# Output projection of an attention layer, halved by heads instead of by columns, with its first sums kept in place

## The chip, the cores and the metric

The kernel runs on one core of one Trainium2 chip. The metric is the device time of one execution in microseconds (us): the median of three runs. A profile of one further execution shows the engines: TensorE (PE; PEld is its weight load), VectorE (DVE), ScalarE (ACT), GpSimd (POOL) and SyncE (SP, which only issues transfers here).

## What is computed

A decoder trunk of two layers on 1024 tokens of width 1024. Layer 0 mixes tokens by a gated short convolution, layer 1 by sparse attention with 16 heads of 128. Behind each mixer stand a residual with layer norm and a mixture of 64 experts (one group of eight, then two experts of it), again with residual and norm. Cut to what matters here:

```python
for i in range(DEPTH):                        # 2
    if i % 2 == 0: m = short_conv_mixer(x, ...)
    else:          m = dsa_mixer(x, ...)      # ends in  o @ w_out,  o: (1024, 2048), w_out: (2048, 1024)
    x = layer_norm(DEEPNORM_ALPHA * x + m, ln1_g[i], ln1_b[i])
    f = hier_moe(x, router_wg[i], router_bg[i], router_we[i], router_be[i], w1[i], w3[i], w2[i])
    x = layer_norm(DEEPNORM_ALPHA * x + f, ln2_g[i], ln2_b[i])
```

## The kernel before

SBUF is an arena of 25 slots of 128 x 2048 numbers (1 MB); `take` and `give` hand them out first in, first out. The order of the work is written out by hand, per engine in program order. Tokens come in 8 tiles of 128.

Matrix products that decide the routing are made of three TensorE passes (`mm3`, L219 to L221): each operand is split into a rounded high part (ScalarE, L207) and the rest (a subtraction, L208, on VectorE or, if the call says so, on GpSimd).

The attention leaves its output in eight slots `Qs[t]`, one per tile, 16 heads of 128 each. The projection then runs over the columns of `w_out` in two halves n of 512, and in each half over the tiles t, in each tile over two head halves q of eight heads. `split_o` splits one head half of one tile (128 x 1024) into one of two buffers `os_[q]`; it is called for each (n, t, q), 32 times. `split_wo` splits the weights, 8 slots for a column half. The first pass (n = 0) keeps its products in `mA` by a ScalarE copy (L1811). The second pass (n = 1) is `mixer`, a generator that `mixer_ln_router` steps through: that function, which layer 0 uses too behind its convolution, loads the residual rows (L411, L414, L465, three buffers `rb`), adds the products (`part`, L427), normalizes the tile before (`norm`, L237 and L242 through `ln_apply`), writes it to DRAM (L444, issued by GpSimd), transposes it (`turn`, L421 and L422) for the router's logits (L557), chooses experts (`route_choice`, L572 to L626) and ranks tokens (`route_rank`, L654 to L687; `table_rows` and `table_slots`, L692 and L698). `fold_router` (L188 to L202) folds the norm's scale into the router's weights during the first tile. `ln_scale` and the line behind it (L230, L231, L433) are small GpSimd operations. Between its steps `prefetch` (L762, on SP) loads expert weights of 1 MB into the slots that are free.

The expert stage (`moe`) takes the experts in 32 pairs; L848 is the activation of a pair. Each layer's experts are 192 loads of 1 MB.

Of the kernel before, what the change touches and what calls it, by code (L numbers as in the profile page):

```python
# [23 lines left out]
F32 = mybir.dt.float32  # L24
# [4 lines left out]
AF = mybir.ActivationFunctionType  # L29
OP = mybir.AluOpType  # L30
# [3 lines left out]
P = 128  # L34
T = 1024
D = 1024
NT = T // P
# [8 lines left out]
ALPHA = 4.0 ** 0.25  # L46
# [3 lines left out]
HEADS = 16  # L50
# [13 lines left out]
MB, EO, EP = 4, -7, 4  # L64


class Net:
# [336 lines left out]
    def mixer_ln_router(self, l, x, mixer, done):  # L404
        nc = self.nc
        rs = [self.take() for _ in range(2)]
        self.rr = None
        *rb, tb = (self.slots[s][:, i * D:(i + 1) * D] for s in rs for i in range(2))
        rb = [rb[t % 3] for t in range(NT)]
        for t in range(2):  # L410
            nc.sync.dma_start(rb[t], x[t * P:(t + 1) * P])  # L411
        self.load_ln(self.i["ln1_g"][l], self.i["ln1_b"][l], nc.sync)
        self.load_router(l)
        nc.sync.dma_start(rb[2], x[2 * P:3 * P])  # L414
        self.route_open()

        def turn(t, h):
# [6 lines left out]
        def part(t, n, ap):  # L424
            s = slice(n * 512, (n + 1) * 512)
            r = rb[t]
            nc.vector.scalar_tensor_tensor(r[:, s], r[:, s], ALPHA, ap, op0=OP.mult, op1=OP.add)  # L427
            self.ln_stats(r, sts[t], n)
            if n:
                st = sts[t]  # L430
                for _ in self.ln_scale(st):
                    pass
                nc.gpsimd.tensor_mul(st[:, 14:15], st[:, 12:13], st[:, 15:16])  # L433
# [18 lines left out]
        last = NT - 1  # L452
        for t in range(NT):
            sts.append(self.small.tile([P, 16], F32, name="st", bufs=3))
            m = mixer(t)
            next(m)
            if t >= 1:
                next(fold, None)
                turn(t - 1, 1)
            g = [self.route_rank(t - 2)] if t >= 2 else []  # L460
            for r in g:
                some(r, FIRST)
            self.run(*([norm(t - 1)] if t >= 1 else []), *g)
# [51 lines left out]
        self.table_slots(t)  # L515
        self.close_slots()
        self.count_all()
        self.give(*rs, self.ln_slot, self.rt, self.rr)


    def route_open(self):
# [676 lines left out]
    def attention(self):  # L1198
        nc, sm, mm = self.nc, self.small, self.nc.tensor.matmul
        w_in, w_out = self.i["attn_w_in"][0], self.i["attn_w_out"][0]  # L1200
        S = self.slots
# [178 lines left out]
        Qs, Q = [], []  # L1380
# [251 lines left out]
        for k, (h, hh) in enumerate(order):  # L1632
# [66 lines left out]
        done = LEAD  # L1699
        raws = {}  # L1700

        def load_wo(n, i):
            r = raws[n, i] = self.take()
            nc.sync.dma_start(S[r].rearrange("p (j c) -> p j c", j=4),
                              w_out[i * 512:(i + 1) * 512, n * 512:(n + 1) * 512].rearrange("(j p) c -> p j c", p=P))

        wos, os_ = {}, []
        chunks = [(n, t, q) for n in range(2) for t in range(NT) for q in range(2)]

        def split_wo(n, i, qs=range(2), eng=None):  # L1710
            r = raws[n, i]
            v = S[r].rearrange("p (j c) -> p j c", j=4)
            for q in qs:
                s = wos[n, 2 * i + q] = self.take()
                o = S[s].rearrange("p (j a c) -> p j a c", j=2, a=2)
                self.split(v[:, 2 * q:2 * q + 2], o[:, :, 0], o[:, :, 1], eng)
            if 1 in qs:
                self.give(raws.pop((n, i)))

        def split_o(c, eng=None):  # L1720
            if c < len(chunks):
                _, t, q = chunks[c]
                self.split(S[Qs[t]][:, q * T:(q + 1) * T], S[os_[q]][:, :T], S[os_[q]][:, T:], eng)

        def project_ahead():

            self.give(*qs, *bs, *mcs[:2], pps[(len(items) - 3) % 3])
            load_wo(0, 2)
            os_.extend(self.take() for _ in range(2))
            split_o(0, nc.gpsimd)  # L1730
            yield
            for i in range(2):
                for q in range(2):
                    split_wo(0, i, (q,), nc.gpsimd if 2 * i + q < EP else None)
                    yield
            load_wo(0, 3)

# [3 lines left out]
        for i in range(len(items)):  # L1741
# [43 lines left out]
        mas = [self.take() for _ in range(2)]  # L1785
        mA = [S[mas[t // 4]][:, (t % 4) * 512:(t % 4 + 1) * 512] for t in range(NT)]
        state = {}

        def project(n, t, q, ks=range(8)):
            if q == 0 and 0 in ks:  # L1790
                state["pt"] = po.tile([P, 512], F32, name="po1")
            o = S[os_[q]]
            for k in (8 * q + k for k in ks):
                w = S[wos[n, k // 2]][:, (k % 2) * T:(k % 2 + 1) * T]
                hs = slice((k % 8) * P, (k % 8 + 1) * P)
                self.mm3(state["pt"], (o[:, :T][:, hs], o[:, T:][:, hs]), (w[:, :512], w[:, 512:]),
                         k == 0, k == HEADS - 1)
            return state["pt"]

        for t in range(NT):  # L1800
            for q in range(2):
                if t == 0 and q == 1:
                    split_wo(0, 2)
                    split_wo(0, 3)
                pt = project(0, t, q)
                split_o(2 * t + q + 1)
                if t == NT - 1:
                    self.give(*[wos.pop((0, 4 * q + i)) for i in range(4)])
                    split_wo(1, 2 * q)
                    split_wo(1, 2 * q + 1)  # L1810
            nc.scalar.activation(mA[t], pt, AF.Copy)  # L1811
            if t < 4:
                load_wo(1, t)

        split_o(2 * NT + 1)

        def mixer(t):
            c = 2 * (NT + t)
            project(1, t, 0, range(2))
            yield  # L1820
            project(1, t, 0, range(2, 8))
            split_o(c + 2, nc.gpsimd)
            if t == NT - 1:
                self.give(*[wos[1, i] for i in range(4)], os_[0])
            yield 0, mA[t]
            if t == 3:
                self.give(mas[0])
            elif t == NT - 1:
                self.give(mas[1])
                self.prefetch(1, 0, AHEAD[1][0])  # L1830
            project(1, t, 1, range(4))
# [8 lines left out]
        self.mixer_ln_router(1, self.xres, mixer, lambda: self.give(*[wos[1, i] for i in range(4, 8)], os_[1]))  # L1840
        ctx.close()


# [63 lines left out]
```

## Time and profile before

| | us |
|---|---|
| median of 3 runs | 2292.85 (2290.36 to 2293.92) |
| profiled execution | 2296.11 |
| its span in the profile | 2294.3 |
| TensorE busy | 2163.9 (94%) |
| VectorE busy | 1179.2 (51%) |
| ScalarE busy | 797.5 (35%) |
| GpSimd busy | 367.7 (16%) |

The profile counts time from the start of the span. Busy time of TensorE is modelled (its matmuls are pipelined), and the granted clock PEclk is a share of full speed, 2.4 GHz; a stretch at 0.83 has parts at 1.2 GHz. Of the span, the convolution's projection loop lies at 290 to 400, the experts of layer 0 at 430 to 910, the attention before 1540, the output projection at 1540 to 1772 (first pass to 1627), the rest of the routing to 1810 and the experts of layer 1 from there to the end.

### The profile page before, as it was taken

What the parts mean: (1) busy time and instruction counts of PE and PEld (TensorE: products, weight loads), DVE (VectorE), ACT (ScalarE), POOL (GpSimd) and SP (SyncE); (2) the same over time, 40 slices, a digit from 0 to 9 for tenths busy, and PEclk for the clock granted to TensorE, in tenths of its full rate; (3) what the DMA queues carried; (4) which work ended last, traced back from release to release, by engine and by line L of the source; (5) the groups of instructions that cost most, each with busy time, mean ns of one, the idle gap of its engine ahead of it and who ended that gap; (6) DMA issues with size and microseconds to landing.
All of it is one profiled execution on the core that took longest, in us unless ns stands there. A gap on an engine that the chain in (4) does not pass through costs nothing. (4 is left out here: it accounts for less than half of the span.)

```text
span 2294.3 us, 32929 instructions
## 1 busy us (share of the span) xinstructions
PE 2163.9 (94%) x12764; PEld 1597.5 (70%) x12764; DVE 1179.2 (51%) x2728; ACT 797.5 (35%) x1626; POOL 367.7 (16%) x435
## 2 busy tenths in 40 slices
PE   8999999799999998799998999999988799999997
PEld 6888888465555654677887899988766455655553
DVE  4333478433333334467888877772688333333333
ACT  3121211222222222356885877762321222222221
POOL 0000011100000001412332633230233100000001
PEclk9999999899999999899998999999988899999999
DMA  5113165699999997221211001010334899999994
GB/s 156 47 56 112 64 249 198 248 418 407 419 419 419 419 419 295 88 55 47 56 28 56 1 2 38 1 62 31 107 129 184 314 418 409 419 419 419 419 420 204
DMA packets 132692, 497.41 MB, mean 217 GB/s; under 512 B 18499, under 2 KB 64787, under 8 KB 82864
## 3 DMA queue, kind: packets, MB, share of 16 engines
q1 hardware_dynamic: 117648, 456.61, 50.6%
q0 software_dynamic: 8496, 34.20, 3.8%
q10 hardware_dynamic: 6384, 4.42, 0.7%
q8 instruction: 102, 1.67, 0.3%
q14 instruction: 62, 0.51, 0.1%
HBM read 474.60 MB, written 19.95 MB: 216 GB/s over the span
## 5 line engine op out<-in xcount | busy, mean ns | idle before, releaser
L840 PE MATMUL ph<-slot,slot 128*64 128x256 f32 x4096 | 456.3, 381 | 7.6 <-DVE nx L741 7.6
L840 PEld LDWEIGHTS ph<-slot,slot 128*64 128x64 f32 x4096 | 296.6, 138 | 183.4 <-issue 45.0
L871 DVE SCALAR_TENSOR_TENSOR slot<-rg,sgate,slot 128x512 fp32r<-128x512 f32 x128 | 96.1, 750 | 288.7 <-ACT slot L870 287.7
L866 PE MATMUL rg<-slot,slot 128*64 128x512 f32 x1024 | 233.8, 598 | 0.9 <-ACT slot L856 0.9
L207 ACT ACTIVATE slot<-slot 128x1024 fp32r<-128x1024 f32 (+3 forms) x169 | 139.5, 873 | 250.3 <-DVE slot L357 147.7
L208 DVE TENSOR_TENSOR slot<-slot,slot 128x1024 fp32r<-128x1024 f32 (+3 forms) x150 | 131.9, 918 | 149.5 <-ACT slot L207 149.5
L219 PE MATMUL ps<-slot,slot 128*128 128x512 f32 x512 | 202.7, 396 | 0.0
L221 PE MATMUL ps<-slot,slot 128*128 128x512 f32 x512 | 199.9, 390 | 0.0
L220 PE MATMUL ps<-slot,slot 128*128 128x512 f32 x512 | 199.8, 390 | 0.0
L219 PE MATMUL po<-slot,slot 128*128 128x256 f32 (+1 forms) x544 | 195.0, 358 | 0.4 <-DVE slot L1622 0.4
L220 PE MATMUL po<-slot,slot 128*128 128x256 f32 (+1 forms) x544 | 186.2, 342 | 0.0
L221 PE MATMUL po<-slot,slot 128*128 128x256 f32 (+1 forms) x544 | 185.8, 342 | 0.0
L230 POOL TENSOR_SCALAR st<-st 128x1 f32<-128x1 f32 x34 | 22.9, 672 | 872.4 <-DVE st L229 791.5
L866 PEld LDWEIGHTS rg<-slot,slot 128*64 128x64 f32 x1024 | 67.8, 136 | 133.5 <-issue 114.6
L870 ACT ACTIVATE slot<-rg,sgate 128x512 fp32r<-128x512 f32 x128 | 88.0, 688 | 203.1 <-PE rg L866 198.4
L848 ACT ACTIVATE slot<-ph 128x256 f32<-128x256 f32 x64 | 24.6, 385 | 379.7 <-PE ph L840 379.7
L849 DVE TENSOR_TENSOR slot<-slot,ph 128x256 f32<-128x256 f32 x64 | 26.9, 420 | 250.4 <-ACT slot L848 250.4
L887 PE MATMUL pc<-slot,slot 128*128 128x512 f32 x512 | 153.0, 420 | 0.4 <-DVE slot L871 0.4
L219 PE MATMUL pa<-slot,slot 128*128 128x512 f32 (+1 forms) x384 | 144.1, 375 | 0.2 <-DVE slot L208 0.2
L221 PE MATMUL pa<-slot,slot 128*128 128x512 f32 (+1 forms) x384 | 143.0, 372 | 0.0
L220 PE MATMUL pa<-slot,slot 128*128 128x512 f32 (+1 forms) x384 | 142.9, 372 | 0.0
L208 DVE TENSOR_TENSOR slot<-pT,slot 128x512 fp32r<-128x512 f32 (+1 forms) x160 | 101.5, 635 | 69.6 <-ACT slot L207 67.7
(304 smaller groups left out, 3891.8 us busy)
## 6 DMA issues: line engine op xcount, KB each, us to landing
slot<-in_exp_w_dram SPq DMA_DIRECT2D x377, 1024.0 KB, 15.9
slot<-in_conv_w_in_dram SPq DMA_DIRECT2D x24, 512.0 KB, 3.8
slot<-in_attn_w_in_dram SPq DMA_DIRECT2D x17, 512.0 KB, 3.7
slot<-in_x_dram SPq DMA_DIRECT2D x16, 512.0 KB, 4.6
slot<-xres SPq DMA_DIRECT2D x16, 512.0 KB, 3.7
slot<-in_attn_w_out_dram SPq DMA_DIRECT2D x8, 1024.0 KB, 8.2
xn<-slot POOLq DMA_DIRECT2D x14, 512.0 KB, 3.1
slot<-in_exp_w_dram POOLq DMA_DIRECT2D x7, 1024.0 KB, 9.8
```

The lines of the kernel that those rows point to most:

```text
L207: self.nc.scalar.activation(hi.bitcast(F32R), raw, AF.Copy)
L208: (eng or self.nc.vector).tensor_sub(lo.bitcast(F32R), raw, hi)
L219: mm(out, ah.bitcast(F32R), bh.bitcast(F32R), start=start, stop=False)
L220: mm(out, ah.bitcast(F32R), bl.bitcast(F32R), start=False, stop=False)
L221: mm(out, al.bitcast(F32R), bh.bitcast(F32R), start=False, stop=stop)
L840: mm(ph[q * CAP:(q + 1) * CAP, m * 256:(m + 1) * 256], gt[k][:, o + q * CAP:o + (q + 1) * CAP], w[:, k * 256:(k + 1) * 256], start=k == 0 ...
L848: nc.scalar.activation(hg, ph[:, :256], AF.Silu)
L849: nc.vector.tensor_mul(hg, hg, ph[:, 256:])
L866: mm(py[q * CAP:(q + 1) * CAP], hT[:, c * P + q * CAP:c * P + (q + 1) * CAP], w[:, c * D + n * 512:c * D + (n + 1) * 512], start=c == 0, s ...
L870: nc.scalar.activation(R_(hi), py, AF.Copy, scale=g)
L871: nc.vector.scalar_tensor_tensor(R_(lo), py, g, hi, op0=OP.mult, op1=OP.subtract)
L887: mm(sums[b, h], R_(pick[i][:, b * P:(b + 1) * P]), R_(S[yslot][:, j * D + h * 512:j * D + (h + 1) * 512]), start=q == 0 and j == 0, stop= ...
```

## The change

The output projection is halved by heads. The first pass takes heads 0 to 7 (q = 0) and makes both column halves of each tile; the second takes heads 8 to 15. Each head half of a tile is then split once, 16 calls of `split_o`, into `os_[c % 2]` by chunk c; in the second pass its subtraction is on VectorE and no longer on GpSimd. Weights are loaded two heads by 1024 columns at a time. The first pass adds ALPHA times the residual, loaded there by `load_x`, to its products (`sums`, on VectorE) and keeps the result in `Qs[t]` in place of heads 0 to 7. `mixer_ln_router` gets these rows: it loads no residual, `part` only adds, and norm and router work in place there; `Qs[t-1]` is given back after its norm. The slots of `mA` go.

```diff
@@ mixer_ln_router
-        rs = [self.take() for _ in range(2)]
         self.rr = None
-        *rb, tb = (self.slots[s][:, i * D:(i + 1) * D] for s in rs for i in range(2))
-        rb = [rb[t % 3] for t in range(NT)]
-        for t in range(2):
-            nc.sync.dma_start(rb[t], x[t * P:(t + 1) * P])
+        if rows:
+            rb, own, *rs, tb = rows
+        else:
...
@@ part
-            nc.vector.scalar_tensor_tensor(r[:, s], r[:, s], ALPHA, ap, op0=OP.mult, op1=OP.add)
+            if rows:
+                nc.vector.tensor_add(r[:, s], r[:, s], ap)
+            else:
+                nc.vector.scalar_tensor_tensor(r[:, s], r[:, s], ALPHA, ap, op0=OP.mult, op1=OP.add)
@@ the loop over tiles
-            if 1 <= t < NT - 2:
+            if rows and t:
+                self.give(own[t - 1])
+            elif 1 <= t < NT - 2:
                 nc.sync.dma_start(rb[t + 2], x[(t + 2) * P:(t + 3) * P])
@@ attention
         def split_o(c, eng=None):
-            if c < len(chunks):
-                _, t, q = chunks[c]
-                self.split(S[Qs[t]][:, q * T:(q + 1) * T], S[os_[q]][:, :T], S[os_[q]][:, T:], eng)
+            if c < 2 * NT:
+                q, t = divmod(c, NT)
+                o = S[os_[c % 2]]
+                self.split(S[Qs[t]][:, q * T:(q + 1) * T], o[:, :T], o[:, T:], eng)
...
+        rs = [self.take() for _ in range(2)]
+        *xb, tb = (S[s][:, i * D:(i + 1) * D] for s in rs for i in range(2))
+        rows_ = [S[Qs[t]][:, :D] for t in range(NT)]
+
+        def load_x(t):
+            if t < NT:
+                nc.sync.dma_start(xb[t % 3], self.xres[t * P:(t + 1) * P])
+
+        def project(c, pt, n, ks=range(8)):
+            q, o = c // NT, S[os_[c % 2]]
+            for k in ks:
+                w = S[wos[q, n, k // 2]][:, (k % 2) * T:(k % 2 + 1) * T]
+                hs = slice(k * P, (k + 1) * P)
+                self.mm3(pt, (o[:, :T][:, hs], o[:, T:][:, hs]), (w[:, :512], w[:, 512:]), k == 0, k == 7)
+
+        def sums(t, n, pt):
+            s = slice(n * 512, (n + 1) * 512)
+            nc.vector.scalar_tensor_tensor(rows_[t][:, s], xb[t % 3][:, s], ALPHA, pt, op0=OP.mult, op1=OP.add)
+
+        for t in range(3):
+            load_x(t)
...
+            else:
+                split_o(t + 1)
+                for n in range(2):
+                    pt = new()
+                    project(t, pt, n)
+                    if t == NT - 1:
+                        self.give(*[wos.pop((0, n, i)) for i in range(4)])
+                        for i in range(4):
+                            split_wo(1, i, (n,))
+                    sums(t, n, pt)
+            load_x(t + 3)
             if t < 4:
                 load_wo(1, t)
...
         def mixer(t):
-            c = 2 * (NT + t)
-            project(1, t, 0, range(2))
+            c = NT + t
+            pt = new()
+            project(c, pt, 0, range(2))
             yield
-            project(1, t, 0, range(2, 8))
-            split_o(c + 2, nc.gpsimd)
+            project(c, pt, 0, range(2, 8))
             if t == NT - 1:
-                self.give(*[wos[1, i] for i in range(4)], os_[0])
-            yield 0, mA[t]
...
+            yield 0, pt
+            split_o(c + 1)
+            pt = new()
+            project(c, pt, 1, range(4))
             yield
-            project(1, t, 1, range(4, 6))
+            project(c, pt, 1, range(4, 6))
             yield
-            pt = project(1, t, 1, range(6, 8))
-            split_o(c + 3, nc.gpsimd)
+            project(c, pt, 1, range(6, 8))
             yield 1, pt
-            self.give(Qs[t])
```

## Rows read from the trace of the kernel before

**Rows 1.** The page's 40 equal slices of the span: GB/s moved.

```profile
GB/s 156 47 56 112 64 249 198 248 418 407 419 419 419 419 419 295 88 55 47 56 28 56 1 2 38 1 62 31 107 129 184 314 418 409 419 419 419 419 420 204
```

**Rows 2.** Stretches: bounds and length, busy us (instructions) per engine, PEclk, DMA share, GB/s.

```profile
320.00:340.00 20.00, 20.00 (x113) 16.76 (x112) 16.92 (x78) 2.95 (x9) 2.39 (x4) 1.00 0.44 159
430.00:435.00 5.00, 5.00 (x31) 3.63 (x31) 1.38 (x2) 2.34 (x4) 0.00 (x0) 1.00 0.00 0
1580.00:1600.00 20.00, 20.00 (x90) 16.58 (x89) 4.13 (x4) 4.26 (x6) 0.00 (x0) 1.00 0.00 0
1700.00:1720.00 20.00, 16.81 (x79) 13.68 (x78) 15.74 (x51) 3.90 (x7) 6.96 (x7) 0.83 0.28 105
1820.00:1840.00 20.00, 20.00 (x140) 11.33 (x136) 2.88 (x6) 2.91 (x6) 0.00 (x0) 1.00 1.02 421
```

**Rows 3.** Line L427: duration ns min/median/max, first to last start us, shape.

```profile
L427 DVE SCALAR_TENSOR_TENSOR slot<-slot,ps x16: 678/681/689, 293.6 to 399.7; 128x512 f32<-128x512 f32 x16
L427 DVE SCALAR_TENSOR_TENSOR slot<-slot,po x8: 676/686/689, 1642.9 to 1771.8; 128x512 f32<-128x512 f32 x8
```

**Rows 4.** TensorE in order of time, a tile of the second pass.

```profile
1707.33 0.67 PE L698 MATMUL pm<-slot 128*128 128x96 f32 x2 [3.19 <-DVE slot L687]
```

**Rows 5.** VectorE in order of time, second pass: start us, us, line, shape.

```profile
1678.57 1.57 DVE L662 TENSOR_TENSOR slot<-slot 128x1 f32<-128x1 f32 x1
1683.69 2.83 DVE L679 SCALAR_TENSOR_TENSOR slot<-slot,v 128x2 f32<-128x2 f32 x1
1698.30 1.85 DVE L662 TENSOR_TENSOR slot<-slot 128x1 f32<-128x1 f32 x1
```

**Rows 6.** GpSimd in order of time: layer 0's loop, then the second pass.

```profile
329.40 0.22 POOL L230 TENSOR_SCALAR st<-st 128x1 f32<-128x1 f32 x1 [9.89 <-DVE slot L654]
330.36 0.97 POOL L433 TENSOR_TENSOR st<-st 128x1 f32<-128x1 f32 x1
...
1677.73 2.39 POOL L208 TENSOR_TENSOR slot<-slot,slot 128x1024 fp32r<-128x1024 f32 x1 [10.01 <-ACT slot L207]
1684.14 2.35 POOL L208 TENSOR_TENSOR slot<-slot,slot 128x1024 fp32r<-128x1024 f32 x1
```

**Rows 7.** VectorE by line, layer 0's loop (308 to 393): busy, mean ns, idle.

```profile
L679 DVE SCALAR_TENSOR_TENSOR slot<-slot,v 128x2 f32<-128x2 f32 x6 | 0.9, 154 | 0.0
```

**Rows 8.** All engines by line, 1500 to 1800: busy us, mean ns, idle before.

```profile
L207 ACT ACTIVATE slot<-slot 128x1024 fp32r<-128x1024 f32 x48 | 49.4, 1056 | 62.8 <-PE po L220 60.4 <-PE po L221 2.4
L208 POOL TENSOR_TENSOR slot<-slot,slot 128x1024 fp32r<-128x1024 f32 x19 | 45.1, 2383 | 84.7 <-ACT slot L207 84.6
```

**Rows 9.** VectorE in order of time: layer 0's loop, then the first pass's end.

```profile
299.28 0.76 DVE L195 TENSOR_TENSOR slot<-slot 128x576 f32<-128x576 f32 x1
299.96 0.68 DVE L427 SCALAR_TENSOR_TENSOR slot<-slot,ps 128x512 f32<-128x512 f32 x1
327.65 0.69 DVE L427 SCALAR_TENSOR_TENSOR slot<-slot,ps 128x512 f32<-128x512 f32 x1 [1.76 <-PE ps L221]
...
1618.02 12.58 DVE L208 TENSOR_TENSOR slot<-slot,slot 128x1024 fp32r<-128x1024 f32 x11 [4.93 <-ACT slot L207]
1640.15 2.81 DVE L195 TENSOR_TENSOR slot<-slot 128x576 f32<-128x576 f32 x1
```

**Rows 10.** ScalarE in order of time: evacuations L1811, activations of expert pairs L848.

```profile
440.51 0.38 ACT L848 ACTIVATE slot<-ph 128x256 f32<-128x256 f32 x1 [5.19 <-PE ph L840]
901.06 0.38 ACT L848 ACTIVATE slot<-ph 128x256 f32<-128x256 f32 x1 [9.97 <-PE ph L840]
...
1616.44 0.60 ACT L1811 ACTIVATE slot<-po 128x512 f32<-128x512 f32 x1 [4.61 <-PE po L221]
1627.32 0.60 ACT L1811 ACTIVATE slot<-po 128x512 f32<-128x512 f32 x1 [0.81 <-PE po L221]
...
1810.82 0.38 ACT L848 ACTIVATE slot<-ph 128x256 f32<-128x256 f32 x1 [5.19 <-PE ph L840]
...
2270.81 0.39 ACT L848 ACTIVATE slot<-ph 128x256 f32<-128x256 f32 x1 [10.00 <-PE ph L840]
```

More of the change, by code (lines that the diff above doesn't have):

```diff
@@ L402, in ln_open, with mixer_ln_router @@
         self.ps_lg = ctx.enter_context(self.tc.tile_pool(name="ps_lg", bufs=1, space=PSUM))
-    def mixer_ln_router(self, l, x, mixer, done):
+    def mixer_ln_router(self, l, x, mixer, done, rows=None):
         nc = self.nc
-        rs = [self.take() for _ in range(2)]
         self.rr = None
-        *rb, tb = (self.slots[s][:, i * D:(i + 1) * D] for s in rs for i in range(2))
-        rb = [rb[t % 3] for t in range(NT)]
-        for t in range(2):
-            nc.sync.dma_start(rb[t], x[t * P:(t + 1) * P])
+        if rows:
+            rb, own, *rs, tb = rows
+        else:
+            rs = [self.take() for _ in range(2)]
+            *rb, tb = (self.slots[s][:, i * D:(i + 1) * D] for s in rs for i in range(2))
+            rb = [rb[t % 3] for t in range(NT)]
+            for t in range(2):
+                nc.sync.dma_start(rb[t], x[t * P:(t + 1) * P])
         self.load_ln(self.i["ln1_g"][l], self.i["ln1_b"][l], nc.sync)
         self.load_router(l)
-        nc.sync.dma_start(rb[2], x[2 * P:3 * P])
+        if not rows:
+            nc.sync.dma_start(rb[2], x[2 * P:3 * P])
         self.route_open()
@@ L517, in mixer_ln_router @@
         self.count_all()
-        self.give(*rs, self.ln_slot, self.rt, self.rr)
+        self.give(*rs, self.ln_slot, self.rt, self.rr, *(own[last:] if rows else ()))
     def route_open(self):
@@ L1700, in attention, with load_wo, split_wo @@
         raws = {}
[L1702 to L1705, printed above, removed]
-        wos, os_ = {}, []
[L1708 to L1714, printed above, removed]
+        def load_wo(q, i):
+            r = raws[q, i] = self.take()
+            h = 8 * q + 2 * i
+            nc.sync.dma_start(S[r].rearrange("p (j c) -> p j c", j=2),
+                              w_out[h * P:(h + 2) * P].rearrange("(j p) c -> p j c", p=P))
+        wos, os_ = {}, []
+        def split_wo(q, i, ns=range(2), eng=None):
+            r = raws[q, i]
+            v = S[r].rearrange("p (j n c) -> p j n c", j=2, n=2)
+            for n in ns:
+                s = wos[q, n, i] = self.take()
                 o = S[s].rearrange("p (j a c) -> p j a c", j=2, a=2)
-                self.split(v[:, 2 * q:2 * q + 2], o[:, :, 0], o[:, :, 1], eng)
-            if 1 in qs:
-                self.give(raws.pop((n, i)))
+                self.split(v[:, :, n], o[:, :, 0], o[:, :, 1], eng)
+            if 1 in ns:
+                self.give(raws.pop((q, i)))
         def split_o(c, eng=None):
-            if c < len(chunks):
-                _, t, q = chunks[c]
-                self.split(S[Qs[t]][:, q * T:(q + 1) * T], S[os_[q]][:, :T], S[os_[q]][:, T:], eng)
+            if c < 2 * NT:
+                q, t = divmod(c, NT)
+                o = S[os_[c % 2]]
+                self.split(S[Qs[t]][:, q * T:(q + 1) * T], o[:, :T], o[:, T:], eng)
         def project_ahead():
@@ L1732, in project_ahead @@
             for i in range(2):
-                for q in range(2):
-                    split_wo(0, i, (q,), nc.gpsimd if 2 * i + q < EP else None)
+                for n in range(2):
+                    split_wo(0, i, (n,), nc.gpsimd if 2 * i + n < EP else None)
                     yield
@@ L1784, in attention @@
         self.ln_open(ctx)
[L1785 to L1798, printed above, removed]
@@ L1800, in attention @@
-        for t in range(NT):
[L1801 to L1811, printed above, removed]
+        rs = [self.take() for _ in range(2)]
@@ new lines, in sums @@
+        def sums(t, n, pt):
[3 more added lines that the diff above has]
+            load_x(t)
+        new = lambda: po.tile([P, 512], F32, name="po1")
+        for t in range(NT):
+            if t == 0:
+                pts_ = [new(), new()]
+                for n in range(2):
+                    project(0, pts_[n], n, range(4))
+                split_wo(0, 2)
+                split_wo(0, 3)
+                split_o(1)
+                for n in range(2):
+                    project(0, pts_[n], n, range(4, 8))
+                    sums(0, n, pts_[n])
+            else:
+                split_o(t + 1)
+                for n in range(2):
+                    pt = new()
[6 more added lines that the diff above has]
+            load_x(t + 3)
@@ L1812, in attention @@
             if t < 4:
                 load_wo(1, t)
-        split_o(2 * NT + 1)
+        self.give(rs[0])
         def mixer(t):
-            c = 2 * (NT + t)
-            project(1, t, 0, range(2))
+            c = NT + t
+            pt = new()
+            project(c, pt, 0, range(2))
             yield
-            project(1, t, 0, range(2, 8))
-            split_o(c + 2, nc.gpsimd)
+            project(c, pt, 0, range(2, 8))
             if t == NT - 1:
-                self.give(*[wos[1, i] for i in range(4)], os_[0])
-            yield 0, mA[t]
[L1826 to L1829, printed above, removed]
+                self.give(*[wos[1, 0, i] for i in range(4)], os_[0])
@@ L1830, in mixer @@
                 self.prefetch(1, 0, AHEAD[1][0])
-            project(1, t, 1, range(4))
+            yield 0, pt
+            split_o(c + 1)
+            pt = new()
+            project(c, pt, 1, range(4))
             yield
-            project(1, t, 1, range(4, 6))
+            project(c, pt, 1, range(4, 6))
             yield
-            pt = project(1, t, 1, range(6, 8))
-            split_o(c + 3, nc.gpsimd)
+            project(c, pt, 1, range(6, 8))
             yield 1, pt
-            self.give(Qs[t])
@@ L1840, in attention @@
-        self.mixer_ln_router(1, self.xres, mixer, lambda: self.give(*[wos[1, i] for i in range(4, 8)], os_[1]))
+        self.mixer_ln_router(1, None, mixer, lambda: self.give(*[wos[1, 1, i] for i in range(4)], os_[1]),
+                             (rows_, Qs, rs[1], tb))
         ctx.close()
```

## Prediction

> **What bounds the kernel now.** I read the page's slices first [rows 1]: the traffic runs at about 419 GB/s in slices 32 to 38, the second expert stage, and falls to 107 to 184 GB/s in slices 28 to 30, where the projection lies. Then the stretches [rows 2], read by stage. In the first pass (1540 to 1627) TensorE is busy for all of each 20 us at granted clock 1.00. In the second pass (1627 to 1772) it is busy for 16.81 of 20 us, VectorE for 15.74, and the granted clock is 0.83, which means that part of the stretch ran at 1.2 GHz and the rest at 2.4. The last stretch shows the expert stage with TensorE and the memory stream both full.
>
> The row to weigh that second pass against is in the same trace. Layer 0 runs the same function `mixer_ln_router` behind its convolution, with the same 48 matmuls of 512 columns per token tile, the same transposes, norm and router, and without a split inside the loop. There TensorE is busy for 20.00 of 20 us at clock 1.00 [rows 2]. The line L427 ends each half tile, so its starts give the period [rows 3, 9]: layer 0's second halves go from 299.96 to 399.7, 99.74 us for 7 tiles, 14.25 us each. Layer 1's go from 1642.9 to 1771.8, 128.9 us for 7, or 18.41 us each.
>
> Next, what makes the difference. In the second pass TensorE's L698 stands 3.19 us waiting for VectorE's L687 [rows 4]. VectorE isn't waiting there: it is inside an instruction on 128x2 numbers that took 2.83 us (L679), and earlier in one on 128x1 that took 1.57 us (L662) [rows 5]. In layer 0 L679 takes 154 ns [rows 7]. GpSimd's rows give the cause [rows 6]: its subtractions of 128x1024 run from 1677.73 to 1680.12 and from 1684.14 to 1686.49; L662 ends at 1680.14 and L679 at 1686.52, within 0.03 us of them. So two subtractions of `split` on GpSimd per tile hold VectorE up, VectorE holds TensorE up, and after TensorE's gap the clock is low for a while. The steady period there is 1698.30 - 1678.57 = 19.73 us [rows 5]: 5.48 over layer 0, of which 3.19 is that wait and some 2.3 the slower clock and smaller waits.
>
> **The change part by part.** *Splits.* Each head half of each tile is split once, not once per column half: 16 ScalarE copies of 1.056 us and their subtractions disappear. The second pass had two per tile, with GpSimd subtractions of 2.38 us [rows 8]. It will have one, with the subtraction on VectorE: 12.58 / 11 = 1.14 to 1.23 us [rows 9]. Where does it stand? It is emitted after `route_choice` and before `part(t, 1)`. In layer 0 VectorE is idle just there, 1.76 us, waiting for TensorE to end the half [rows 9]. The copy goes ahead of it on ScalarE, behind the two small exponentials, while VectorE ends the choice; the buffer alternates by tile, so it has no one to wait for. I therefore cost it at 0, with 0.53 us to spare. If the cover is gone it costs at most 1.23 x 7 = 8.6 us. A gain from it is excluded, since TensorE is full.
>
> On the moved subtraction a rule speaks against the change. In layer 0 GpSimd's L433, a 128x1 product, takes 0.97 us where VectorE's norm runs beside it [rows 6]. The Trainium skill, SBUF — State Buffer, section "SBUF: two separate sides", says that VectorE and GpSimd share one port pair as a lock for a whole instruction, in both directions; a VectorE operation with two inputs in SBUF shuts a reading GpSimd out. The trace agrees with both directions. By the rule the moved subtraction could hold GpSimd up, and the sum would be 2271 with it. In layer 0 GpSimd is idle before L230 for 9.89 us [rows 6], which covers that place; my sum has 0, and the case is counted with the first rival.
>
> *Loop of the second pass.* With GpSimd's subtractions gone, its dependencies are those of layer 0: `part(t, 0)` now waits for a product in PSUM and not for a saved one, as there. The period goes from 18.41 to 14.25: 7 x 4.16 = 29.1 us less. In tile 0 the router's L195 took 2.81 us beside GpSimd, and the first measured half started right behind it; in layer 0 it takes 0.76 [rows 9]. That is 2.05 less. Together 31.2.
>
> *First pass.* A tile takes 1627.32 - 1616.44 = 10.88 us, 48 matmuls at 0.227, with nothing else on the path [rows 10]. The matmuls stay 768 in all. Per tile one VectorE subtraction (1.23) and one ScalarE copy go, and so does the 0.60 us evacuation; two sums of about 0.69, each reading PSUM (L427's form), come. VectorE was busy for 4.13 of 20 us [rows 2], so nothing waits. Each sum has the 5.44 us of the next half to free its buffer. Cost 0; without cover it would be 16 x 0.69 = 11 us, which I exclude by that room. At the turn to the second pass eight weight splits share VectorE with the last two sums. Eleven of these took 12.58 us from 1618.02 [rows 9]; four of them and a split end at about 1623.7, the sum at 1624.4, and the buffer is wanted at 1627.3. The last sum lands near 1629.7, wanted at 1632.7. Cost 0.
>
> *Queues.* SP issues eight residual loads in the first pass, three at its start, the others each behind its sum and two tiles ahead. The loads of the output weights queue behind them, and are wanted only in tile 7. In the second pass SP has expert loads alone: the waits for a norm's write to DRAM move from the residual loads to the expert loads that reuse those rows. Seven slots of the arena's 25 are given a tile later, three others are free from the start, so one expert load more is out at the loop's end: a gain of at most 2.5 us (1.05 MB at 419 GB/s), taken as 0, because the stream stands still before the expert stage anyway.
>
> *What follows the loop.* From the last L427 to the first L848 layer 0 took 440.51 - 399.7 = 40.8 us and layer 1 1810.82 - 1771.8 = 39.0 [rows 3, 10]. After the change loads and gathers will lie as in layer 0, so between 0 and 1.8 us comes back; I take 0.9. Then the 32 expert pairs: 901.06 - 440.51 = 460.55 and 2270.81 - 1810.82 = 459.99 [rows 10]. That stage takes the same time after a loop of 14.25 and one of 18.41, so an earlier start is an earlier end.
>
> Sum: 29.1 + 2.05 - 0.9 = 30.3 us. The profiled execution, 2296.11 us (span 2294.3, 1.8 around it), becomes 2265.8. The median shown is 3.26 us below that execution; I take the same distance: 2262.5.
>
> **The rivals.** *VectorE has no room.* If the split's subtraction ends after TensorE's half, TensorE waits. Against it: 1.76 us of idle for 1.23. For it: VectorE is busy for 16.92 of 20 us in layer 0 [rows 2], and the spare is 0.53. It decides once the subtraction starts 0.53 us late. Price: 8.6 us, and if each gap also brings the low clock, 2.3 a tile more, 7 x 3.53 = 24.7: 2271 to 2287. A GpSimd chain held up by the moved subtraction costs the same 1.23 a tile and decides when the two meet; I give it 2 of this rival's 8%.
>
> *The expert stream sets the end.* If the expert stage hangs on bytes and not on its start, only the one more load counts: 2292.85 - 2.5 = 2290. For it: the stream is full from 1820 on. Against it: just before layer 0's first pair it runs at 0 GB/s [rows 2], with every slot filled, though the loop there takes 14.25 a tile; and the equal lengths of the two stages. It decides if slots are still empty when the first pair starts. The Trainium skill, same page, section "A bandwidth-pool intuition that's wrong", calls HBM almost always the bottleneck and gives 358 GB/s for a core; the trace shows 421 [rows 2], so that its figure doesn't hold here.
>
> *Slower: the long instructions aren't GpSimd's doing.* If L662 and L679 stay long for another reason, as the reuse of the score rows or the router's own chain, the period stays 18.41 and VectorE gets the 1.23 on top: 2292.85 + 8.6 = 2301.5. It decides if these lines stay above 1 us without a GpSimd subtraction beside them. Against it: 154 ns in layer 0, and ends that agree to 0.03 us.
>
> **How the numbers follow.** Forecast 80%, no room 8%, stream 8%, slower 4%. The forecast's own range is 2260 (the extra load) to 2263.4 (the whole 1.8), widened to 2257 by the spread of 3.6 us of the runs shown. Upwards the range goes to 2273, the first rival without the clock and its 1.8. About 0.2%, 4.6 us, is what a measurement can tell: faster 0.88 (forecast and first rival), same 0.08, slower 0.04.
>
> **What would show it.** L427's period near 14.2 us at clock 1.00; L662, L679 and L195 at 0.16, 0.16 and 0.76 us; no 128x1024 subtraction on GpSimd in the loop; L698 without a wait; the last L427 near 1741; 460 us of expert pairs. A low clock in that loop, or VectorE's L208 ending when TensorE already waits, would be the first rival; an expert stage over 480 us the second.

## The result, and the profile after

| | before | after |
|---|---|---|
| median, us | 2292.24 (2290.36 to 2293.92, 4 runs) | 2262.26 (2260.43 to 2263.60, 4 runs) |
| ratio of the medians | | 0.987 (0.9859 to 0.9882) |
| profiled execution, us | 2296.11 | 2261.69 |
| its span, us | 2294.3 | 2259.8 |

The kernel is 30.0 us shorter; the interval of the ratio makes that 27.0 to 32.3 us. The new lines shift the numbers: L427 is now L433 (in layer 1), L421 is L426, L662, L679, L687 and L698 are L672, L689, L697 and L708, the sums of the first pass are L1815, and the activation of an expert pair, L848, is L858.

The same stretches as in [rows 2], by stage: bounds and length, busy us (instructions) of PE, PEld, DVE, ACT and POOL, granted clock, DMA share, GB/s.

```profile
1580.00:1600.00 20.00, 20.00 (x90) 16.57 (x89) 5.20 (x6) 2.12 (x2) 0.00 (x0) 1.00 0.30 105
1700.00:1720.00 20.00, 20.00 (x116) 16.96 (x116) 17.99 (x79) 4.51 (x11) 2.40 (x4) 1.00 0.43 150
1765.00:1770.00 5.00, 5.00 (x27) 3.79 (x27) 1.79 (x3) 1.91 (x4) 0.00 (x0) 1.00 0.02 7
1770.00:1775.00 5.00, 5.00 (x50) 3.31 (x47) 0.00 (x0) 1.16 (x1) 0.00 (x0) 1.00 0.25 51
```

In the second pass (1700 to 1720) TensorE is busy for all 20 us at clock 1.00, where it had 16.81 at 0.83 [rows 2]. The stretch now looks like layer 0's loop. The first pass is as full as it was, with 5.20 us on VectorE in place of 4.13. The stretches at 1765 and 1770, just before and at the start of the experts, matter below: hardly anything is being loaded there.

Two lines by their sources: durations in ns (min, median, max), first and last start.

```profile
L433 DVE TENSOR_TENSOR slot<-slot,po x16: 680/684/690, 1629.6 to 1737.3; 128x512 f32<-128x512 f32 x16
L858 ACT ACTIVATE slot<-ph x64: 383/384/388, 438.2 to 2236.5; 128x256 f32<-128x256 f32 x64
```

VectorE by line in the loop (1645 to 1735): busy us, mean ns of one, idle before it.

```profile
L208 DVE TENSOR_TENSOR slot<-slot,slot 128x1024 fp32r<-128x1024 f32 x6 | 7.3, 1218 | 0.0
...
L672 DVE TENSOR_TENSOR slot<-slot 128x1 f32<-128x1 f32 x6 | 1.0, 160 | 0.0
...
L689 DVE SCALAR_TENSOR_TENSOR slot<-slot,v 128x2 f32<-128x2 f32 x6 | 0.9, 154 | 0.0
```

The two instructions that took 1.57 to 2.83 us [rows 5] take 160 and 154 ns. VectorE in order of time shows the turn between the passes, tile 0 and a split in the loop:

```profile
1619.79 0.68 DVE L1815 SCALAR_TENSOR_TENSOR slot<-slot,po 128x512 f32<-128x512 f32 x1
...
1624.99 0.68 DVE L1815 SCALAR_TENSOR_TENSOR slot<-slot,po 128x512 f32<-128x512 f32 x1
1629.56 0.69 DVE L433 TENSOR_TENSOR slot<-slot,po 128x512 f32<-128x512 f32 x1 [3.88 <-PE po L221]
...
1636.94 0.76 DVE L195 TENSOR_TENSOR slot<-slot 128x576 f32<-128x576 f32 x1
1637.62 0.68 DVE L433 TENSOR_TENSOR slot<-slot,po 128x512 f32<-128x512 f32 x1
...
1663.37 0.16 DVE L636 TENSOR_TENSOR slot<-gates,slot 128x2 f32<-128x2 f32 x1
1663.45 1.22 DVE L208 TENSOR_TENSOR slot<-slot,slot 128x1024 fp32r<-128x1024 f32 x1
1665.31 0.69 DVE L433 TENSOR_TENSOR slot<-slot,po 128x512 f32<-128x512 f32 x1 [0.64 <-PE po L221]
```

L195 is down from 2.81 to 0.76. The split (1663.45 to 1664.67) fits into the gap before the second half's sum, and 0.64 us of the gap is left. ScalarE has its copy, and later the first expert pair:

```profile
1661.89 1.04 ACT L207 ACTIVATE slot<-slot 128x1024 fp32r<-128x1024 f32 x1
...
1776.36 0.38 ACT L858 ACTIVATE slot<-ph 128x256 f32<-128x256 f32 x1 [5.20 <-PE ph L850]
```

GpSimd's chain of the norm, in order of time, has nothing of 128x1024 beside it and takes what it took in layer 0 [rows 6]:

```profile
1681.23 0.22 POOL L230 TENSOR_SCALAR st<-st 128x1 f32<-128x1 f32 x1 [9.97 <-DVE slot L664]
1681.53 0.57 POOL L231 TENSOR_TENSOR st<-st,mhalf 128x1 f32<-128x1 f32 x1
1682.18 0.97 POOL L441 TENSOR_TENSOR st<-st 128x1 f32<-128x1 f32 x1
```

Where the time went, profile against profile, 34.5 us of span:

| stretch | before | after | saved |
|---|---|---|---|
| start to the projection's first matmul | 1539.95 | 1536.74 | 3.2 |
| from there to tile 0's second half | 102.93 | 100.88 | 2.05 |
| seven tiles of the second pass | 128.87 | 99.73 | 29.14 |
| last sum to the first expert pair | 39.07 | 39.01 | 0.06 |
| first to last pair | 459.99 | 460.15 | -0.16 |
| last pair to the end of the span | 23.5 | 23.3 | 0.2 |

The first row is no work of the change: 2.3 of its 3.2 us stand already at layer 0's first pair (440.51 [rows 10] against 438.23), and 3.15 at a ScalarE line early in the attention (L1425, now L1435, first at 1070.01 against 1066.86). The profiled execution of before was simply 3.9 us over its median, that of after 0.6 under its own. What the change touches is 31.2 us, all in the second pass.

### The profile page after: what moved, and what is told of

Same layout as the page of the kernel before. It is cut to its first block, busy times and chain, and to the rows that moved or that the text cites. A ratio compares the mean times of both kernels' runs of the same rounds, so it can differ in the third digit from the quotient of the medians.

```text
span 2259.8 us, 32870 instructions
## 1 busy us (share of the span) xinstructions
PE 2148.8 (95%) x12764; PEld 1586.2 (70%) x12764; DVE 1164.3 (52%) x2742; ACT 776.4 (34%) x1602; POOL 334.8 (15%) x420
## 5 line engine op out<-in xcount | busy, mean ns | idle before, releaser
L850 PE MATMUL ph<-slot,slot 128*64 128x256 f32 x4096 | 456.5, 381 | 7.6 <-DVE nx L751 7.6
L850 PEld LDWEIGHTS ph<-slot,slot 128*64 128x64 f32 x4096 | 296.1, 138 | 184.1 <-issue 46.5
L207 ACT ACTIVATE slot<-slot 128x1024 fp32r<-128x1024 f32 (+3 forms) x153 | 123.6, 854 | 251.9 <-DVE slot L357 147.8
L219 PE MATMUL po<-slot,slot 128*128 128x256 f32 (+1 forms) x544 | 189.9, 349 | 0.4 <-DVE slot L1632 0.4
L221 PE MATMUL po<-slot,slot 128*128 128x256 f32 (+1 forms) x544 | 181.6, 334 | 0.0
L220 PE MATMUL po<-slot,slot 128*128 128x256 f32 (+1 forms) x544 | 181.4, 334 | 0.0
L230 POOL TENSOR_SCALAR st<-st 128x1 f32<-128x1 f32 x34 | 22.9, 672 | 949.9 <-DVE st L229 794.2
L858 ACT ACTIVATE slot<-ph 128x256 f32<-128x256 f32 x64 | 24.6, 385 | 380.0 <-PE ph L850 380.0
```

Of the source, the lines that this page charges most:

```text
L207: self.nc.scalar.activation(hi.bitcast(F32R), raw, AF.Copy)
L219: mm(out, ah.bitcast(F32R), bh.bitcast(F32R), start=start, stop=False)
L220: mm(out, ah.bitcast(F32R), bl.bitcast(F32R), start=False, stop=False)
L221: mm(out, al.bitcast(F32R), bh.bitcast(F32R), start=False, stop=stop)
L850: mm(ph[q * CAP:(q + 1) * CAP, m * 256:(m + 1) * 256], gt[k][:, o + q * CAP:o + (q + 1) * CAP], w[:, k * 256:(k + 1) * 256], start=k == 0 ...
L858: nc.scalar.activation(hg, ph[:, :256], AF.Silu)
```

## The experiments

Three questions. Is it GpSimd's subtractions that held VectorE, and how much is the hold, how much the clock? Is it the engine of the split that counts, or its place? And how far are the two rivals, no room and the stream, from deciding? "us" is the median. The period is that of the second halves. Before has 128.87 us for seven tiles, after 99.73, some 14.2 us a tile.

**Two GpSimd subtractions put back.** After, with two unused subtractions of 128x1024 on GpSimd in each tile of the second pass, one before each half's sum. A ScalarE copy of 512 columns of the half's product sets their time.

```diff
-        self.give(rs[0])
+        X = S[rs[0]]
+
+        def load_pool(c, pt):
+            nc.scalar.activation(X[:, :512], pt, AF.Copy)
+            nc.gpsimd.tensor_sub(X[:, T:], S[os_[c % 2]][:, :T], X[:, :T])
...
+            load_pool(c, pt)
             yield 0, pt
...
+            load_pool(c, pt)
             yield 1, pt
...
+        self.give(rs[0])
```

`X` is a scratch slot that after gives back before the loop and this kernel behind it; the other runs with `X` below do the same. Three such slots fewer for the loads cost nothing (the last runs below).

> The changed kernel, and per tile of the second pass two more GpSimd subtractions of 128x1024 into a scratch slot, each released by a ScalarE copy (0.6 us) at the end of a half tile, as the two of before were. They are extra work that the result doesn't use. Theory (GpSimd's subtractions hold VectorE): L662's and L679's successors take over 1 us again, the period of half tiles goes from 14.24 back to 18.4 (17.5 to 19), clock about 0.85, time 2262.3 + 7 x 4.2 = 2291 (2286 to 2296). Rival (the gain is the smaller number of splits on the path, or the rows in place): period 14.2 to 14.4, time 2262 to 2264.

Measured: 2283.70 us (2277.44 to 2288.35), ratio 0.9963 (0.995 to 0.9975). That is less than the 2286 to 2296 that were expected; by the medians 21.4 of the 30.0 us are gone again. GpSimd, VectorE and TensorE in one tile, each in order of time:

```profile
1683.16 2.40 POOL L1848 TENSOR_TENSOR slot<-slot,slot 128x1024 f32<-128x1024 f32 x1 [7.71 <-ACT slot L1847]
...
1689.59 2.35 POOL L1848 TENSOR_TENSOR slot<-slot,slot 128x1024 f32<-128x1024 f32 x1
```

```profile
1684.93 0.65 DVE L672 TENSOR_TENSOR slot<-slot 128x1 f32<-128x1 f32 x1
...
1689.66 2.51 DVE L697 TENSOR_TENSOR slot<-slot 128x192 fp32r<-128x192 bf16 x1
```

```profile
1692.23 0.42 PE L708 MATMUL pm<-slot 128*128 128x96 f32 x2 [1.82 <-DVE slot L697]
```

The chain of before is back: L672 ends at 1685.58, the subtraction beside it at 1685.56; L697, 0.35 us by itself, takes 2.51 and ends 0.23 behind the second subtraction; TensorE's L708 waits 1.82 us for it. The victims differ from those of before, because the subtractions start at other moments, so the copy is not exact.

The clock is the part that differs. In the profiled execution the loop took 114.28 us, 14.6 more than after. Stretches behind two of its waits, that of 1.82 us ending at 1692.23 and the next, of 1.80 us, ending at 1708.75:

```profile
1692.00:1697.00 5.00, 4.77 (x24) 3.91 (x24) 4.53 (x22) 1.01 (x4) 0.00 (x0) 1.00 0.61 210
...
1707.00:1712.00 5.00, 3.25 (x9) 2.67 (x10) 4.64 (x12) 0.00 (x0) 1.48 (x1) 0.66 0.58 179
1712.00:1717.00 5.00, 5.00 (x29) 3.98 (x28) 3.52 (x19) 2.08 (x5) 0.00 (x0) 1.00 0.26 108
```

Equal waits, but the granted clock is 1.00 behind the first and 0.66 behind the second, for less than 5 us. The profiled execution is the shortest of the six, and the mean clock goes with the time: 0.978 in it, 0.972 in the longest. So the other 6 us of the median are likely a clock that fell behind more of these waits; no trace of a longer execution shows it.

**The same load without reading.** The same, but with an instruction that only writes.

```diff
-            nc.gpsimd.tensor_sub(X[:, T:], S[os_[c % 2]][:, :T], X[:, :T])
+            nc.gpsimd.iota(X, pattern=[[1, 2 * T]], base=0, channel_multiplier=0, ...)
```

> As the run with two more GpSimd subtractions per tile (2283.7 us), with each replaced by a GpSimd iota of 128x2048 into the scratch slot, which writes SBUF and reads nothing; same release, near 1.8 us each. If what costs is GpSimd's queue (L230 behind a long instruction) or its writes: about three quarters of the 21 us, 2278 (2274 to 2282). If VectorE's operations with two SBUF inputs are held only by a GpSimd operation that reads: L672 back at 0.16 us and the period at 14.3 to 14.6, 2263 to 2266.

Measured: 2265.32 us (2264.29 to 2266.03), ratio 0.9878 (0.9862 to 0.9895). GpSimd and VectorE in tile 0, first in this run, with the write, then in the run above, with the subtraction:

```profile
1637.66 1.84 POOL L1848 IOTA slot<- 128x2048 f32 x1 [4.45 <-ACT slot L1847]
```

```profile
1638.02 0.76 DVE L195 TENSOR_TENSOR slot<-slot 128x576 f32<-128x576 f32 x1
```

```profile
1634.63 2.38 POOL L1848 TENSOR_TENSOR slot<-slot,slot 128x1024 f32<-128x1024 f32 x1 [3.90 <-ACT slot L1847]
```

```profile
1634.99 2.63 DVE L195 TENSOR_TENSOR slot<-slot 128x576 f32<-128x576 f32 x1
```

L195, with two inputs in SBUF, lies wholly inside the write and takes 0.76 us, as in after; beside the subtraction it takes 2.63. L582 does likewise: 0.28 us inside a write (1689.53, the write at 1688.18 to 1690.02), 1.09 and 1.20 beside subtractions. GpSimd is occupied 1.84 us at a time, twice a tile, by 2048 written columns, the copies of ScalarE are there, and none of VectorE's instructions in the loop is drawn out. 3.1 us remain for the occupied queue and the copies. So what holds VectorE is not that GpSimd is busy, nor that it writes, but the subtraction, which reads. The medians alone would not show it: the writes are shorter and fall beside other instructions (L672 starts at 1683.70, 0.06 us before its write ends, and L697 before its write starts), so part of the 18.4 us between the two runs may come of where they fall. The Trainium skill, SBUF — State Buffer, section "SBUF: two separate sides", says that a VectorE operation with two inputs in SBUF is locked out only against a GpSimd operation that reads SBUF; L195 at 0.76 us here and at 2.63 beside the subtraction agree with it.

**The hold without TensorE's gap.** Before, with matmuls into a PSUM tile that nobody reads, put where TensorE waits for L687.

```diff
                 self.table_rows(t - 2)
+                if l:
+                    self.warm(self.psw, "wm", self.g_t[:, :512], 3)
                 self.table_slots(t - 2)
...
+        self.psw = ctx.enter_context(self.tc.tile_pool(name="ps_w", bufs=1, space=PSUM))
```

> The kernel before with three unused matmuls of 0.85 us put on TensorE ahead of L698, where it stood idle for 3.19 us in a tile; they are extra work that only keeps it busy. Theory: the wait ends as before, but the granted clock stays at 2.4 GHz behind it, and the 2.3 us a tile that I put down to the clock go: 6 x 2.3 = 14 us, 2278 (2274 to 2284), clock over 0.95 in the loop. If the low clock lies beside VectorE's work and costs nothing: 2292. If the fill outlasts the wait: over 2292.

Measured: 2282.99 us (2282.53 to 2285.37), ratio 0.9961 (0.9947 to 0.9975). TensorE, then VectorE, then a stretch (L681, L689 and L700 are before's L679, L687 and L698):

```profile
1712.77 2.82 PE L89 MATMUL wm<-slot,ident 128*128 128x512 f32 x6
1715.84 0.42 PE L700 MATMUL pm<-slot 128*128 128x96 f32 x2 [0.24 <-DVE slot L689]
```

```profile
1712.21 2.84 DVE L681 SCALAR_TENSOR_TENSOR slot<-slot,v 128x2 f32<-128x2 f32 x1
```

```profile
1700.00:1720.00 20.00, 19.76 (x100) 15.22 (x100) 18.11 (x65) 4.18 (x10) 6.96 (x6) 1.00 0.39 153
```

VectorE is held as long as before (2.84 us), but TensorE has something to do in that time, the clock is 1.00, and the loop takes 119.63 us, not 128.87. Matmuls that do nothing useful make this kernel 9.0 us faster, where 14 were expected. The low clock was thus worth some 9.2 us of the loop, less whatever the fill itself costs; a piece of it is left in tile 0 (0.66 at 1640 to 1645). The remaining 119.63 - 99.73 = 19.9 us are the hold and what else differs between the two kernels.

**The engine alone.** Before, with both subtractions of the second pass on VectorE, at the places where they were.

```diff
-            split_o(c + 2, nc.gpsimd)
+            split_o(c + 2)
...
-            split_o(c + 3, nc.gpsimd)
+            split_o(c + 3)
```

> The kernel before with the two subtractions per tile of the second pass on VectorE and no longer on GpSimd; still 32 splits and columns halved. Theory: L662 and L679 fall to 0.16 us, but each subtraction now stands in VectorE's queue ahead of the sum and waits for TensorE's end of the half and the copy (1.06 us): period between 14.25 and 18.4, near 16.5, time 2279 (2270 to 2290). If the engine of the subtraction alone makes the gain: 2262. If the halved count alone makes it: 2292 or more, by 7 x 2.46 us up to 2309.

Measured: 2275.48 us (2273.93 to 2276.06), ratio 0.9921 (0.9904 to 0.9938): 16.5 of the 30.0 us. The loop takes 111.03 us. ScalarE, VectorE and TensorE around one split:

```profile
1686.05 1.06 ACT L207 ACTIVATE slot<-slot 128x1024 fp32r<-128x1024 f32 x1 [1.46 <-PE po L221]
```

```profile
1687.14 1.23 DVE L208 TENSOR_TENSOR slot<-slot,slot 128x1024 fp32r<-128x1024 f32 x1 [1.49 <-ACT slot L207]
1688.28 0.68 DVE L427 SCALAR_TENSOR_TENSOR slot<-slot,po 128x512 f32<-128x512 f32 x1
```

```profile
1689.02 0.66 PE L421 MATMUL tr<-ident,slot 128*128 128x128 f32 x4 [1.76 <-DVE slot L427]
```

A new chain: the copy waits for the matmuls that read the same buffer, the subtraction for the copy, the half's sum stands behind the subtraction in VectorE's queue, and TensorE's transposes wait for the sum, 1.46 to 1.76 us a tile. The granted clock was 1.00 over the whole loop (1640 to 1750) all the same.

**The place alone.** After, with its one subtraction per tile on GpSimd.

```diff
-            split_o(c + 1)
+            split_o(c + 1, nc.gpsimd)
```

> The changed kernel with its one split per tile in the second pass subtracting on GpSimd again. Theory: the subtraction of 2.4 us starts when the ScalarE copy ends and holds the last small operations of the expert choice, some 2 us; VectorE then has the 1.22 us of its own subtraction free and 0.64 us of idle, so that the period stays between 14.25 and 14.9: 2262 to 2267 us. If each GpSimd subtraction costs its whole length wherever it stands: 2262.3 + 7 x 2.4 = 2279. If the gain came from taking the work off GpSimd at all, as before: half of the 30 us is lost, 2277.

Measured: 2262.92 us (2261.80 to 2265.11), ratio 0.9872 (0.9855 to 0.9888), as after; the loop takes 100.58 us. GpSimd, then VectorE:

```profile
1663.02 2.39 POOL L208 TENSOR_TENSOR slot<-slot,slot 128x1024 fp32r<-128x1024 f32 x1 [5.86 <-ACT slot L207]
```

```profile
1663.16 2.28 DVE L634 CAST slot<-gates 128x2 fp32r<-128x2 f32 x1
1665.47 0.16 DVE L636 TENSOR_TENSOR slot<-gates,slot 128x2 f32<-128x2 f32 x1
1665.55 0.68 DVE L433 TENSOR_TENSOR slot<-slot,po 128x512 f32<-128x512 f32 x1
```

VectorE is held here too, 2.28 us at a conversion of 128x2. But the hold falls into the 1.9 us that VectorE has free before the half's sum, and costs 0.85 us in seven tiles. In the new place, with the alternating buffer and one split a tile, the engine hardly matters.

**How much room there is.** After, with one and with two unused VectorE subtractions behind the split.

```diff
             split_o(c + 1)
+            for _ in range(2):   # 1 in the first kernel
+                nc.vector.tensor_sub(X[:, T:], S[os_[c % 2]][:, :T], X[:, :T])
...
```

> The changed kernel with one unused subtraction of 128x1024 more per tile on VectorE, right behind the split's. Theory (the split lies in idle time): 1.22 us meets 0.64 us of idle before the half's sum and some 0.5 us until TensorE needs that sum: 0 to 0.3 us a tile, 2262 to 2265. If VectorE has no room at all: 7 x 1.22 = 8.5, 2271.

> The changed kernel with two unused subtractions more per tile behind the split's: 2.44 us into 0.64 of idle and about 0.5 of slack. Theory: 1.3 us a tile on TensorE, which is too short a wait for the clock to fall (it stayed at 1.00 with waits of 1.6 to 1.8 us): period 15.5, 2262.3 + 7 x 1.3 = 2271 (2268 to 2275). If the rival of a low clock holds for such a wait: 2 us a tile more, 2287. If VectorE has room for these too: 2263.

Measured: 2265.03 us (2264.78 to 2265.85) with one, 2273.04 (2270.68 to 2273.88) with two; the loop 102.32 and 111.15 us, a tile 14.5 and 15.8. TensorE with one, then with two:

```profile
1681.75 0.66 PE L426 MATMUL tr<-ident,slot 128*128 128x128 f32 x4 [0.17 <-DVE slot L433]
```

```profile
1685.34 0.66 PE L426 MATMUL tr<-ident,slot 128*128 128x128 f32 x4 [1.42 <-DVE slot L433]
```

Of the first one's 1.22 us a tile, 0.64 are the rest of VectorE's gap, and another 0.47 lie between the sum's end and TensorE's transposes (in after, 1666.00 and 1666.47); it costs 2.8 us in all. The second costs 8.0, 1.14 a tile, nearly its whole length. The clock stayed at 1.00 in the loop; the expectation's ground for that left out the wait of 1.80 us above, behind which it fell. A second split's subtraction at the new place would thus cost 2.8 us, and this is what halving the count is worth there, without the second ScalarE copy, which was not added. In the old place two on VectorE stand 13.2 us above after. So 2275.48 - 2265.03 = 10.45 of these go with what else differs: the place, the buffer that alternates and the first half's sum fed from PSUM above all. These were not taken apart.

**Loads later.** After, with the expert loads of the second pass held back to tile 5.

```diff
-            if t < last:
+            if t < last and (not rows or t >= 5):
                 self.prefetch(...)
```

> The changed kernel with no expert load issued after tiles 0 to 4 of the second pass; the slots free by then are filled from tile 5 on. Seven loads go out later, none is left out. Theory (all slots are full before the first pair anyway): 2262.3, within 2 us. If the stream sets the end and early loads count: up to 7 x 2.5 = 17 us, 2280.

Measured: 2262.73 us (2259.72 to 2263.92), ratio 0.9866 (0.985 to 0.9883). It tells nothing: nothing else is queued on SP that could hold the loads until tile 5, and they were issued at the moment they were in after (from 1630.4 against 1630.2). The next two take the slots instead.

**Fewer slots for the loads.** After, with three free slots kept out of the loads' reach until the loop is over; and the same with the seven row slots also given back only behind the routing.

```diff
+        hold = [self.take() for _ in range(3)]
         self.mixer_ln_router(1, None, mixer, ...)
+        self.give(*hold)
... the second kernel besides:
-            if rows and t:
-                self.give(own[t - 1])
...
-        self.give(*rs, self.ln_slot, self.rt, self.rr, *(own[last:] if rows else ()))
+        self.give(*rs, self.ln_slot, self.rt, self.rr, *(own if rows else ()))
```

> The changed kernel with three free slots held back until the end of the routing, so that three expert loads of 1 MB go out only behind the loop. In the run before, later calls of the prefetch moved nothing: SP has nothing else in its queue and issued the loads at the same times. Theory (the stream stands still for some 10 us before the first pair, in which 7.5 us of loads find room): 2262.3 to 2265. If the stream sets the end and early loads count: 3 x 2.5 = 7.5, 2270.

> As the run before, and the eight slots of the rows too are given back only behind the routing: ten loads less go out during the loop, 25 us of stream at 419 GB/s. Between the loop's end and the first pair lie 39 us, in which the changed kernel still moves about 9 MB (22 us) and gathers rows. Theory: 47 us of stream do not fit into 39, so that here early loads begin to count: 5 to 15 us later, 2267 to 2277. If the start of the experts alone sets the end: 2262. If all early loads count: 2262.3 + 25 = 2287.

Measured: 2263.95 us (2261.95 to 2264.58) with three, ratio 0.9878 (0.9862 to 0.9895); 2273.67 (2272.32 to 2276.34) with ten, ratio 0.9924 (0.9907 to 0.994). At the loop's last sum SP has issued 15 expert loads in after (14 in before), 12 with three slots held and 6 with ten, so that nine loads are missing there and not ten. With three, the stretches before the first pair:

```profile
1765.00:1770.00 5.00, 5.00 (x27) 3.78 (x27) 1.58 (x3) 1.89 (x4) 0.00 (x0) 1.00 1.01 421
1770.00:1775.00 5.00, 5.00 (x50) 3.33 (x48) 0.00 (x0) 1.19 (x1) 0.00 (x0) 1.00 0.62 205
```

421 GB/s where after moves 7: the three loads come at the end and not during the loop, and still the first pair starts at 1776.38 and the last at 2236.59, as in after. With ten, the first pair starts at 1776.22, the last at 2246.37, ten us later. TensorE by line from 1960 on (this L848 is after's L850), busy us, mean ns, idle and its releaser:

```profile
L848 PE MATMUL ph<-slot,slot 128*64 128x256 f32 x1216 | 138.9, 383 | 5.7 <-DMA slot<-in_exp_w_dram 5.7
```

Here the expert stage waits for its loads, though not at its start: up to the pair at 2042.97 each is as early as in after, then the lead is used up. In after the same line has no idle time. The stream sets the end, then, once some number of loads between four and nine is missing at the loop's end. After has at least three to spare.

## Why the prediction held, step by step

The forecast was 2262.5 us and the median is 2262.26. Its mechanism is the one that the runs show. That the two agree to 0.24 us is luck: the four runs of after lie 3.2 us apart, and two errors of the sum, below, offset each other. The sizes, one by one:

- *The loop, 29.1.* 29.14 by the profile, 14.1 to 14.3 us a tile and 15.2 in the last, clock 1.00, L672 and L689 at 0.16 and 0.15 us. Layer 0's loop was the right row to weigh it against.
- *L195, 2.05.* 2.81 to 0.76, and tile 0's second half is 2.05 earlier within the pass.
- *What follows the loop, minus 0.9.* Mis-sized: 0.06 us the other way. Between the ends 0 and 1.8 the prediction took the middle on the ground that loads would lie as in layer 0. They do (7 GB/s before the first pair), and the stretch still took 39.0 us; why layer 0 has 1.8 more was not tested.
- *The split in VectorE's gap, 0.* Right, with 0.64 us to spare where 0.53 was reckoned. The case of the moved subtraction holding GpSimd up (2271) did not come: GpSimd is idle for 9.97 us before L230, as in layer 0, and L441 takes 0.97 as there.
- *First pass and turn, 0.* Right: TensorE full at 1580 to 1600. At the turn the two last sums start at 1619.79 and 1624.99. With the 3.2 us by which all lies earlier that is 1623.0 and 1628.2, against 1624.4 and 1629.7 reckoned, and VectorE then idles for 3.88 us.
- *The extra load, at most 2.5, taken as 0.* Right by the three-slot run: 15 loads are out where before had 14, as forecast, and three fewer move the first and last pair by under 0.1 us.
- *Profile to median.* The sum of 30.3 was right to 0.3 for the medians (30.0), and was made against one execution, from which 3.26 was taken off. Against the profiled execution of after, 2261.69, its 2265.8 is 4.1 too long: 0.9 of that is the tail, and 3.2 lies before the projection. That the earlier stretch ran long in the one profiled execution is what the 3.26 took account of, in one number and without knowing where. By the two profiles the change is worth 31.2 us and by the medians 30.0; the tail, booked at 0.9 too much, brought the sum nearer to the medians by chance.
- *The range.* Its lower end, 2260 less the spread of 3.6 us, is 2256.4 and not 2257; nothing hangs on it.

The rivals. *No room* is refuted, and its price was too high in one part: the prediction let each gap bring the low clock at 2.3 us a tile. With waits of 1.3 to 1.5 us a tile the clock stayed at 1.00, and the loop grew by 11.4 us, not 24.7. The clock's own price was some 9.2 us in before's whole loop, 1.3 a tile, and not 2.3 (a figure that held the smaller waits too). *The stream* is refuted for this kernel and true with ten slots held. *Slower* is refuted twice: the lines are short without GpSimd's subtractions, and long again with them.

Put together, of 30.0 us: the low clock 9, the hold of VectorE and the split's place some 20 (with 2.05 at L195), of which halving the number of splits is about 2.8 by its subtractions. These are differences between kernels and need not add up exactly.

## What to carry to other kernels

When an instruction on a few numbers takes microseconds, look at which instruction of the engine beside it ends in the same moment, and try that one's place or its engine before its own code. An engine that is free is no free place for work: the subtractions cost GpSimd nothing and the kernel some 20 us, while the same work cost nothing in a gap of VectorE or of GpSimd that TensorE's half left open. A stage of the same trace that runs the same code without the suspect was the better estimate here: layer 0's loop gave the gain of this one to 0.1 us, while adding up one tile's waits put the clock at 2.3 us a tile where 1.3 was measured.

## What the runs showed of the hardware

- GpSimd's subtraction held VectorE's operations with two inputs in SBUF to its end (within 0.03 us at L672; L195 took 2.63 us); its pattern write of 1.84 us did not (L195 took 0.76). The other way round, GpSimd's 128x1 product L441 took 0.97 us beside VectorE's L237 of 128x1024 (in after, 1682.18) and 0.19 with VectorE idle (1740.91). Operations with a single input were held as well: a conversion of 128x2 (2.28 us where it takes 0.17), and in after's tail a 128x8 operation with a scalar (L593 at 1742.53, 1.93 us where it takes 0.23, its end within 0.03 us of that of a GpSimd product of 128x1024). Beside the subtraction of 1683.16 the statistics of 128x512 (L225 at 1683.83, 0.69 us), a product with one input in PSUM (L664 at 1684.69, 0.11) and a 128x1 operation with a scalar (L670 at 1684.84, 0.15) kept their lengths.
- TensorE's granted clock stayed at 1.00, its level of 2.4 GHz, through waits of 1.3 to 1.8 us in tile after tile. But some waits of that length were followed by its level of 1.2 GHz: one of 1.80 us (5 us at 0.66, above), and one of 1.73 us in tile 0 of before, ending at 1643.61 (0.69 at 1643 to 1648). Behind waits of 2.7 to 3.2 us the stretches of before had 0.83 to 0.91, which means that parts of them ran at 1.2 GHz. No run shows what tells the two kinds of short wait apart. Filling the long wait with unused matmuls paid 9.0 us.
